# z as a fourth kind of the seven-product scheme, and a quarter of the off-diagonal low parts on GpSimd, in a two-layer encoder trunk on one core

## The chip, the cores and the metric

One core of a Trainium2 chip. The engines named below are TensorE (PE, with PEld for its weight loads), VectorE (DVE), ScalarE (ACT), GpSimd (POOL) and SyncE (SP, whose queue issues the DMAs of this kernel). The metric is the device time of one execution in microseconds, as the median of three runs. All work is on this core; there is no other core to wait for.

## The reference, cut to what matters

A stream of 2048 tokens with 1024 channels goes through two layers. Layer 0 is a pooling mixer with a gate; from its result keys and values are made once. Layer 1 is a strictly causal stick-breaking attention with 16 heads of 64, whose output is multiplied by SiLU(z). In layer 1 q and z come from one projection of the same normed stream:

```python
h = rms_norm(x, b_norm[j])
q, z = jnp.split(h @ b_w_in[j], 2, axis=-1)          # 1024 channels each
q = rms_norm(split_heads(q), b_q_norm[j])
o = stick_breaking_attention(q, k_sh, v_sh)          # keys s < t only
x = x + (o * jax.nn.silu(z)) @ b_w_out[j]
x = x + (p[i] @ ple_w[i]) * jax.nn.sigmoid(x @ ple_gate_w[i])
```

Everything is fp32. The kernel reaches that accuracy with fp32r matmuls: each operand is split into a high part (a cast to fp32r, on ACT) and a low part (the fp32 value minus the high part, on VectorE or GpSimd), and each product takes three matmuls: high by high, high by low, low by high.

## The kernel before, in words

**Tiling.** The stream lies transposed, channels in the partitions, in four chunks (0 to 3) of 512 tokens. A row is 128 channels x 512 tokens; a chunk of 1024 channels has eight rows. A product of a chunk with a 1024 x 1024 weight is 8 x 8 tiles x 3 matmuls = 192 matmuls of 128x128 by 128x512.

**Stages, in the order in which they run.** Mixer of chunk 0 (`mixed_part`), its gate (`gated_part`), mixer of chunk 1, gate of chunk 1, then `pair_part(0, 1)`, which makes v, k and q of both chunks; then the first attention (`attend` over chunks 0 and 1, 48 slots); gate of chunk 3; `pair_part(2, 3)`; the second attention (chunks 2 and 3, 112 slots); the last chunk's output (`post(3)`). What is left over runs as a filler stream between the matmuls of the attentions: in the first one z of chunks 0 and 1 (`z_part`, `gate_z`, 192 matmuls for each chunk), the mixer and gate of chunk 2 and the mixer of chunk 3 (`beside_first`); in the second one z of chunks 2 and 3 and the outputs of chunks 0 to 2 (`beside_second`). A number of filler matmuls for each half step of the attention (`share`) spreads them evenly.

**The seven products.** For v, k and q of two chunks the kernel takes the 2x2 block product with seven multiplications instead of eight (`job`): products p1 to p7 with 48 matmuls each and 12 multiply-adds of tiles behind them, so 336 matmuls for each kind and pair of chunks instead of 384. It needs mixtures of the weight's four blocks and of the stream's four blocks. The stream's mixtures (`prefill`, `build`) are made at the start of each pair. The weight's mixtures are made once, in `mixtures()`, as a side job of chunk 1's mixer: a step loads four blocks of 128x512 on SP's queue into four `mx` tiles, ACT scales them by the gain, VectorE or GpSimd by turns makes four differences in place, and four stores put them into DRAM (`mixed[kind, name]`). The `mx` tiles share eight buffers (`ppt`) with the attention's `pp` tiles. A kind has four steps. The results of a kind are handed on by `evacuate`, `valued` (v) and `keyed` (k, q; heads are normed there and transposed on TensorE).

**Weights on their way to TensorE.** All weight tiles of dense products come as units: a DMA into `wraw`, a cast into `wpair` on ACT (L208), a low part, and for some a store of the split form, which later uses load again. `take` and `plan` set which unit is loaded ahead of which.

**A half step of the attention.** A slot is one head of one chunk against one key chunk, taken from the diagonal down. `front` makes the scores of a block of 128 queries by 512 keys (ACT's sigmoid into `pp`, L1141, then a running product along the keys as a scan on VectorE, L1145); `turn`, three half steps later, transposes a block of 128 keys by 512 queries on TensorE into the bank `psa`, takes the high part by a cast on ACT (`at`, L1163) and the low part by a subtract on VectorE (L1165); `gather`, one half step on, multiplies both parts with the values (`pso`). Each half step has two of each, and a slot takes two half steps.

**What sets the order.** In the pairs and the attentions (`hold`) TensorE's instructions keep the order of the code; all else is ordered by a scheduler, and each engine runs its list in that order. SP's queue is in order, too. Work that is put off (`after`, `late`, `store(n)`) falls n matmuls later in the list.

## Time and profile before

| | value |
|---|---|
| median of 3 runs | 2713.84 us (2712.88 to 2716.44) |
| profiled execution | 2712.43 us, span 2710.6 us, mean granted clock 0.992 |
| TensorE matmul | 2645.2 us busy, 98% |
| TensorE weight load | 2202.2 us, 81% |
| VectorE | 2040.2 us, 75% |
| ScalarE | 1464.7 us, 54% |
| GpSimd | 903.6 us, 33% |
| DMA | 630.76 MB, 233 GB/s on average |

How to read it: the rows of a stage give start and end in microseconds from the span's start, then the busy time and the number of instructions of PE, PEld, DVE, ACT, POOL and SP's DMA issues. A row of the timeline gives start, duration, engine, line, operation, out<-in and shapes, how many in a row (x), and in square brackets the wait ahead of it and what ended it. A row of the waits reads: who waited, at which line, for whom; total us, times, longest one.

### The profile page before, as it was taken

Reading aid. Unit: us, or ns where it says so; the run is one execution under the profiler, and the core shown is the slowest. Engines: PE = TensorE matmul, PEld = TensorE weight load, DVE = VectorE, ACT = ScalarE, POOL = GpSimd, SP = SyncE. Lnnn points to the kernel's source line nnn. Section 1 sums busy time; section 2 is a strip of 40 time slices with the busy share of each in tenths; the row PEclk is TensorE's granted clock in tenths of the full one; section 3 lists DMA queues with packets and bytes.
Section 4 is the critical chain, followed back from the end, with each engine's and each line's share of the span. In section 5 each row is a group of like instructions: output and inputs, shape, how many; then the busy total and the mean of one; then the engine's idle time right before and its main releaser. Section 6 shows DMA issues by size and latency. Waiting matters only on the chain.

```text
span 2710.6 us, 38493 instructions
## 1 busy us (share of the span) xinstructions
PE 2645.2 (98%) x13118; PEld 2202.2 (81%) x13118; DVE 2040.2 (75%) x2663; ACT 1464.7 (54%) x2906; POOL 903.6 (33%) x685
## 2 busy tenths in 40 slices
PE   9999999999899999999999999999999999999999
PEld 7888887788678887888878787888888888888887
DVE  6744768567857878797576668889988888899842
ACT  5442354466676547555444656666665555555531
POOL 1235554576643414542445766110100100010000
PEclk9999999999999999999999999999999999999999
DMA  6768995957998766866459678755665565556564
GB/s 250 266 231 282 364 315 158 309 170 238 360 353 302 267 229 205 295 219 238 151 158 296 189 221 292 274 188 185 204 230 175 187 214 183 183 171 233 169 201 155
DMA packets 315361, 630.76 MB, mean 233 GB/s; under 512 B 47646, under 2 KB 80414, under 8 KB 315164
## 3 DMA queue, kind: packets, MB, share of 16 engines
q1 hardware_dynamic: 314588, 627.51, 69.2%
q8 instruction: 104, 1.70, 0.3%
q14 instruction: 93, 0.76, 0.1%
q10 hardware_dynamic: 576, 0.79, 0.1%
HBM read 463.03 MB, written 165.15 MB: 232 GB/s over the span
## 4 chain that ended last, share of the span: by engine, by line
PE 57%; DVE 13%; DMA 6%; issue 4%; POOL 4%; ACT 2%; SPq 1%; DVEq 0%; ACTq 0%; POOLq 0%
PE psd L51 26%; PE pso L51 8%; PE psl L51 7%; PE psa L55 7%; DVE pp L1145 4%; PE total L51 4%; PE own L51 4%; DVE at L1165 2%; POOL rq L181 1%; DVE wpair L210 1%; DMA wraw<-in_gate_a_dram 1%; PE pst L55 1%; DMA xw<-x2d 1%; DVE us L576 1%; DMA wraw<-in_w_kv_dram 1%
## 5 line engine op out<-in xcount | busy, mean ns | idle before, releaser
L1145 DVE TENSOR_TENSOR_SCAN pp<-pp,floor 128x512 f32<-128x512 f32 (+3 forms) x640 | 739.5, 1193 | 2.2 <-ACT pp L1141 2.1
L51 PE MATMUL psd<-x,wpair 128*128 128x512 f32 x2304 | 574.0, 395 | 1.3 <-ACT sg L718 0.6
L1163 ACT CAST at<-psa 128x512 fp32r<-128x512 f32 (+3 forms) x640 | 303.9, 525 | 386.2 <-PE psa L55 384.7
L51 PEld LDWEIGHTS psd<-x,wpair 128*128 128x128 f32 x2304 | 433.5, 190 | 94.3 <-ACT sg L718 1.0
L1165 DVE TENSOR_TENSOR at<-psa,at 128x512 fp32r<-128x512 f32 (+3 forms) x640 | 360.0, 600 | 146.6 <-ACT at L1163 145.0
L51 PE MATMUL psd<-xp,wpair 128*128 128x512 f32 x1392 | 337.3, 392 | 1.8 <-DMA wpair<-wf 1.5
L51 PE MATMUL pso<-at,vv 128*128 128x512 f32 (+3 forms) x1280 | 319.3, 367 | 17.2 <-DVE at L1165 13.2
L1141 ACT ACTIVATE pp<-psl 128x512 f32<-128x512 f32 (+3 forms) x640 | 312.8, 549 | 4.1 <-PE psl L51 3.5
L51 PEld LDWEIGHTS psd<-xp,wpair 128*128 128x128 f32 x1392 | 258.7, 188 | 57.6 <-DMA wpair<-wf 1.9
L55 PE MATMUL psa<-ident,pp 128*128 128x128 f32 x2176 | 293.1, 274 | 4.9 <-DVE at L1165 3.7
L51 PEld LDWEIGHTS pso<-at,vv 128*128 128x128 f32 x1280 | 229.8, 188 | 78.7 <-DVE at L1165 29.1
L51 PE MATMUL total<-wpair,xs 128*128 128x512 f32 x1152 | 278.2, 397 | 3.4 <-DVE wpair L210 1.7
L55 PEld LDWEIGHTS psa<-ident,pp 128*128 128x128 f32 x2176 | 253.2, 141 | 33.7 <-DVE at L1165 5.3
L1188 POOL TENSOR_TENSOR os<-os,zt 128x512 f32<-128x512 f32 x32 | 51.0, 1593 | 683.5 <-ACT os L1187 674.4
L51 PE MATMUL psl<-kk,qa 128*128 128x512 f32 (+3 forms) x640 | 259.8, 410 | 3.7 <-ACT pp L1141 3.6
L51 PEld LDWEIGHTS total<-wpair,xs 128*128 128x128 f32 x1152 | 215.3, 190 | 52.5 <-DVE wpair L210 4.2
L210 DVE TENSOR_TENSOR wpair<-wraw,wpair 128x512 fp32r<-128x512 f32 x193 | 176.9, 938 | 98.2 <-ACT wpair L208 97.9
L51 PE MATMUL psl<-kk,qb 128*128 128x512 f32 (+3 forms) x640 | 235.6, 368 | 6.9 <-ACT qb L1108 6.9
L51 PE MATMUL own<-wpair,xs 128*128 128x512 f32 x864 | 209.0, 397 | 7.7 <-ACT qs L938 7.7
L51 PEld LDWEIGHTS own<-wpair,xs 128*128 128x128 f32 x864 | 162.3, 190 | 42.6 <-ACT qs L938 9.4
L51 PE MATMUL psd<-og,wpair 128*128 128x512 f32 x744 | 184.6, 390 | 0.0
L51 PE MATMUL psd<-mp,wpair 128*128 128x512 f32 x768 | 178.8, 390 | 0.0
(151 smaller groups left out, 3657.8 us busy)
## 6 DMA issues: line engine op xcount, KB each, us to landing
wpair<-once SPq DMA_DIRECT2D x288, 512.0 KB, 4.8
kk<-kd SPq DMA_DIRECT2D x160, 256.0 KB, 3.5
vv<-vd SPq DMA_DIRECT2D x160, 256.0 KB, 3.3
once<-wpair SPq DMA_DIRECT2D x48, 512.0 KB, 6.3
wpair<-wf SPq DMA_DIRECT2D x48, 512.0 KB, 5.7
xw<-x2d SPq DMA_DIRECT2D x72, 256.0 KB, 4.5
once<-kp SPq DMA_DIRECT2D x36, 512.0 KB, 4.6
wraw<-in_gate_a_dram SPq DMA_DIRECT2D x64, 256.0 KB, 3.2
```

The costliest lines, as they stand in the source:

```text
L51: return held_in_order(nc.tensor.matmul(*a, **k))
L55: return held_in_order(nc.tensor.transpose(*a, **k))
L181: G.tensor_tensor(out=out_ap, in0=ms, in1=neghalf[:, 0:w], op=ALU.pow)
L210: (V if state["solo"] or state["lo"] % 2 else G).tensor_tensor(out=pr[:, 1], in0=raw, in1=f(pr[:, 0]), op=ALU.subtract)
L576: V.tensor_tensor(out=us[:, lo:][:, ::-1], in0=cur[:, lo:][:, ::-1], in1=cur[:, lo - sh : n][:, ::-1], op=ALU.add)
L1141: A.activation(out=pp[:, r0:], in_=ps[:, :w], func=AF.Sigmoid, scale=-1.0)
L1145: V.tensor_tensor_scan(out=pp[:, r0:][:, ::-1], data0=pp[:, r0:][:, ::-1], data1=least, initial=1.0 if st["diag"] else st["carry"][j], op0 ...
L1163: A.copy(out=at[:, 0, cs], in_=pt[:, cs])
L1165: return lambda: V.tensor_tensor(out=at[:, 1, cs], in0=pt[:, cs], in1=f(at[:, 0, cs]), op=ALU.subtract)
L1188: G.tensor_tensor(out=os, in0=os, in1=zt, op=ALU.mult)
```

## The change

z becomes a fourth kind (`KINDS = "vkqz"`): its four products are made in the pairs by the seven-product scheme, with the weight tile as the stationary operand, and `opened` takes SiLU and stores it. `mixtures()` therefore has 16 steps instead of 12, spaced 35 matmuls apart instead of 46, still as a side job of chunk 1's mixer. `z_part`, `gate_z`, `reload` and `plan_z` go, and with them 384 filler matmuls from each attention, so `share` falls. `prep(2)` (loading chunk 2's stream, splitting it and summing its squares), which ran beside z of chunk 1, moves to the end of `pair_part(0, 1)`, with its low parts on VectorE; loads of the first chunk's heads for the outputs move to the end of `pair_part(2, 3)`. In chunks 2 and 3, in blocks off the diagonal, the low part of the fourth key block (kt == 3) is made by GpSimd from a copy of the bank that ACT takes into a `pp` tile that is done with. The value differences go from GpSimd to VectorE.

```diff
@@ -264
-    KINDS = "vkq"
+    KINDS = "vkqz"
...
     def plan_kinds():
         for kind in KINDS:
-            src, gain = {"q": (b_w_q, g_b), "k": (w_kv, g_kv), "v": (w_kv, g_kv)}[kind]
+            src, gain = {"z": (b_w_z, g_b), "q": (b_w_q, g_b), "k": (w_kv, g_kv), "v": (w_kv, g_kv)}[kind]
...
@@ -433
-            ck[nm] = row("acc") if nm == "acc1" else pool.tile([P, W5], F32, tag="acc", name="acc", bufs=1)
+            ck[nm] = row("acc") if nm == "acc1" and ck is not chunk[2] else pool.tile([P, W5], F32, tag="acc", name="acc", bufs=1)
@@ -530
-            split(pr, xin, G)
+            split(pr, xin, V if state["hold"] and state["solo"] else G)
...
-        if state["solo"]:
+        if not state["hold"]:
             ck["rb1"] = bcast(token_norm(ck["acc1"], "x"), "x")
             return
@@ -667
-                x1 = xr
+                x1 = row("x1")
                 if whole is not None:
-                    x1 = row("x1")
                     whole.append(x1)
@@ -741
     def differences(s, b, j, vr, vs):
-        G.tensor_tensor(out=vs, in0=vs, in1=vr, op=ALU.subtract)
+        V.tensor_tensor(out=vs, in0=vs, in1=vr, op=ALU.subtract)
@@ -811
-    def gate_z(s, acts):
...
+    def opened(s, half, m, zr):
+        sg = tmp("sg")
+        A.activation(out=sg, in_=zr, func=AF.Sigmoid)
+        V.tensor_tensor(out=zr, in0=zr, in1=sg, op=ALU.mult)
+        store(16, out=zd[s][m + 4 * half], in_=zr)
@@ -877
-        for name in ("p5", "p3", "p7", "p6", "p4"):
+        for name in ("p3", "p5", "p7", "p6", "p4"):
             sets[name] = [home(8 + i) if name == "p6" and i < 3 else pair("xs") for i in range(4)]
@@ -909
     def mixtures():
...
-            src, gain = {"q": (b_w_q, g_b), "k": (w_kv, g_kv), "v": (w_kv, g_kv)}[kind]
+            src, gain = {"z": (b_w_z, g_b), "q": (b_w_q, g_b), "k": (w_kv, g_kv), "v": (w_kv, g_kv)}[kind]
@@ -930
     def evacuate(c0, c1, kind, name, j, total, own, parts):
...
+            elif kind == "z":
+                opened(c, b, j, qs)
@@ -973
-                            T.matmul(ps, half_of(sets[name][i], xh)[:, tk], u[:, wh, 0],
+                            xs, w = half_of(sets[name][i], xh), u[:, wh, 0]
+                            if kind == "z":
+                                xs, w = w, xs
+                            T.matmul(ps, xs[:, tk], w,
@@ -981
-    def reload(s):
...
@@ -1015
-    def pair_part(c0, c1):
+    def pair_part(c0, c1, back, width):
...
-        back = reload(c0)
...
-            if n >= total - 96 and n % 10 == 0:
+            if n >= total - width and n % 12 == 0:
                 next(back, None)
@@ -1052
-        yield from mixed_part(1, mixtures(), 46)
+        yield from mixed_part(1, mixtures(), 35)
         yield from gated_part(1, prefill(0), 26)
-        yield from pair_part(0, 1)
+        yield from pair_part(0, 1, prep(2), 140)
+
+    def head_loads():
+        for n in range(1, KT + 1):
+            load_heads(0, n)
+            yield
 
     def beside_first():
-        yield from z_part(0, reload(1))
-        yield from z_part(1, prep(2))
         yield from mixed_part(2)
...
     def middle():
         yield from gated_part(3, prefill(2), 26)
-        yield from pair_part(2, 3)
+        yield from pair_part(2, 3, head_loads(), 100)
 
     def beside_second():
-        yield from z_part(2, reload(3))
-        yield from z_part(3)
         for c in range(NSUB - 1):
             yield from post(c)
@@ -1162
-        return lambda: V.tensor_tensor(out=at[:, 1, cs], in0=pt[:, cs], in1=f(at[:, 0, cs]), op=ALU.subtract)
+        if st["c"] < 2 or st["diag"] or kt < 3:
+            return lambda: V.tensor_tensor(out=at[:, 1, cs], in0=pt[:, cs], in1=f(at[:, 0, cs]), op=ALU.subtract)
+        raw = st["a"][3][0]
+        A.copy(out=raw, in_=pt)
+        return lambda: G.tensor_tensor(out=at[:, 1], in0=raw, in1=f(at[:, 0]), op=ALU.subtract)
@@ -1267
-    attend(0, FIRST, beside_first(), lambda n: (1776.0 - 44) / (2 * FIRST + LAG_G + 1))
+    attend(0, FIRST, beside_first(), lambda n: (1392.0 - 44) / (2 * FIRST + LAG_G + 1))
...
-           lambda n: (1680.0 - 44) / (2 * (len(slots) - FIRST) + LAG_G + 1))
+           lambda n: (1296.0 - 44) / (2 * (len(slots) - FIRST) + LAG_G + 1))
@@ -1315
-        "b_w_z": blocks(b_in[:, 1024:], 256),
+        "b_w_z": blocks(b_in[:, 1024:], 512),
```

In numbers of instructions: TensorE issues 96 matmuls fewer. ACT gets 80 copies of a bank and 16 scalings of `mx` more, and 32 casts of x fewer. VectorE gives up 80 low parts of `at` and takes 32 value differences; GpSimd the other way round. SP issues 32 loads of z's mixtures, 16 loads of blocks and 16 stores more, 48 loads and 16 stores of split z units and 32 reloads of the stream fewer.

Three places in the order. In the rows `x3` stands for three in a row.

First, ACT at the start of chunk 1's gate (L208 is the cast of a weight unit, L188 the cast of a high part, `mx<-mx,gains` the scaling of a mixture step's blocks; the gate's products go to `psd` and its first output is the sigmoid `sg<-psd`). Before:

```order
L921 ACTIVATE mx<-mx,gains 128x512
L188 CAST x_3642<-xr 128x512
L921 ACTIVATE mx<-mx,gains 128x512 x3
L208 CAST wpair<-wraw 128x512 x3
L921 ACTIVATE mx<-mx,gains 128x512 x2
L208 CAST wpair<-wraw 128x512
L921 ACTIVATE mx<-mx,gains 128x512 x2
L188 CAST x_3693<-xr 128x512
L188 CAST ple<-pin 128x512 x2
L208 CAST wpair<-wraw 128x512 x2
L718 ACTIVATE sg<-psd 128x512 x2
```

After, from behind the first activations of z's second step (the casts of the gate's first three units stand some rows ahead of this):

```order
L188 CAST xs<-xw 128x512
L884 ACTIVATE mx<-mx,gains 128x512
L188 CAST xs<-xw 128x512
L884 ACTIVATE mx<-mx,gains 128x512
L188 CAST xs<-xw 128x512
L884 ACTIVATE mx<-mx,gains 128x512
L188 CAST xs<-xw 128x512
L884 ACTIVATE mx<-mx,gains 128x512 x4
L208 CAST wpair<-wraw 128x512 x2
L884 ACTIVATE mx<-mx,gains 128x512 x4
L208 CAST wpair<-wraw 128x512 x4
L709 ACTIVATE sg<-psd 128x512
```

The casts of the gate's fourth unit and of the first ple unit, which stood among the last steps of q, now stand behind the first of the two full sets of four `mx` activations (z's second step), and the next four casts behind the second (z's third step).

Second, SP's queue at the same place (L70 is a store, L917 or L880 the load of a mixture step's block, L225 the load of a weight unit). Before:

```order
L917 DMA mx<-in_b_w_q_dram 128x512
L225 DMA wraw<-in_gate_a_dram 128x512
L70 DMA mixedqp_383<-mx 128x512
L917 DMA mx<-in_b_w_q_dram 128x512
L70 DMA mixedqp_381<-mx 128x512
L917 DMA mx<-in_b_w_q_dram 128x512
L70 DMA mixedqp_384<-mx 128x512
L225 DMA wraw<-in_gate_a_dram 128x512
L917 DMA mx<-in_b_w_q_dram 128x512
L225 DMA wraw<-in_ple_a_dram 128x512
L225 DMA wraw<-in_gate_a_dram 128x512 x2
L70 DMA x2d_0_141<-sg 128x512
```

After:

```order
L70 DMA mixedqp_384<-mx 128x512
L70 DMA mixedzp_386<-mx 128x512
L70 DMA mixedzp_387<-mx 128x512
L880 DMA mx<-in_b_w_z_dram 128x512
L70 DMA mixedzp_385<-mx 128x512
L880 DMA mx<-in_b_w_z_dram 128x512 x2
L70 DMA mixedzp_388<-mx 128x512
L880 DMA mx<-in_b_w_z_dram 128x512 x5
L70 DMA mixedzp_386<-mx 128x512
L225 DMA wraw<-in_gate_a_dram 128x512
L70 DMA mixedzp_387<-mx 128x512
L225 DMA wraw<-in_gate_a_dram 128x512
```

Where two gate loads stood among q's last step, two gate loads now stand behind stores of z's mixtures (`mixedzp`), which go out only when the step's differences are made.

Third, ACT and GpSimd in the second attention (L1120 is the new line of the cast of `at`, L1125 the copy of the bank, L1126 GpSimd's subtract). ACT before:

```order
L1163 CAST at<-psa 128x512 x2
L1141 ACTIVATE pp<-psl 128x512 x2
L1163 CAST at<-psa 128x512 x2
L1141 ACTIVATE pp<-psl 128x512 x2
L1163 CAST at<-psa 128x512 x2
L1141 ACTIVATE pp<-psl 128x512 x2
```

ACT after:

```order
L1120 CAST at<-psa 128x512 x2
L1125 COPY pp<-psa 128x512
L1098 ACTIVATE pp<-psl 128x128
L1098 ACTIVATE pp<-psl 128x256
L1120 CAST at<-psa 128x512 x2
L1098 ACTIVATE pp<-psl 128x384
L1098 ACTIVATE pp<-psl 128x512
L1120 CAST at<-psa 128x512 x2
L1125 COPY pp<-psa 128x512
L1098 ACTIVATE pp<-psl 128x512 x2
```

GpSimd after:

```order
L1126 TENSOR_TENSOR at<-pp,at 128x512 x4
L1149 TENSOR_TENSOR os<-os,zt 128x512
L189 TENSOR_TENSOR op<-os,op 128x512
L1126 TENSOR_TENSOR at<-pp,at 128x512 x4
L1149 TENSOR_TENSOR os<-os,zt 128x512
L189 TENSOR_TENSOR op<-os,op 128x512
```

The copy follows the two casts of its half step, ahead of the next sigmoids; on GpSimd the subtracts stand in the same list as the products with z (`os<-os,zt`) and the low parts of the outputs.

58 lines of the change are left out of this document (7 added, 51 removed).

## The prediction

> **What bounds the kernel now.** I read the page first, then the busy time stage by stage, then who TensorE waits for.
>
> ```profile
> PE 2645.2 (98%) x13118; PEld 2202.2 (81%) x13118; DVE 2040.2 (75%) x2663; ACT 1464.7 (54%) x2906; POOL 903.6 (33%) x685
> ...
> 229.50:364.30 134.80, 133.29 (x593) 109.69 (x592) 83.72 (x95) 44.90 (x72) 66.25 (x59) 1.00 0.95 348
> 364.30:419.80 55.50, 55.07 (x241) 44.74 (x240) 47.09 (x46) 31.49 (x56) 36.80 (x25) 1.00 0.80 257
> 688.70:1337.40 648.70, 623.98 (x3157) 522.91 (x3156) 491.49 (x633) 378.13 (x806) 269.20 (x206) 0.99 0.75 263
> 1651.00:2607.00 956.00, 941.82 (x5058) 793.92 (x5057) 850.43 (x1041) 574.55 (x1190) 98.40 (x61) 0.99 0.61 201
> ...
> PE pso L51 <- DVE at L1165: 13.2, 16, 1.9
> PE pst L55 <- DVE at L1165: 5.9, 6, 2.4
> PE pst L51 <- POOL acc L441: 3.8, 2, 2.4
> ```
>
> A stage's row gives its length, then the busy time of PE, PEld, DVE, ACT and POOL, the clock, the DMA share and GB/s. TensorE is the bound nearly everywhere; its longest entry of waits is 13.2 us in the whole run. Two stages have a second resource close behind. In 229.5 to 364.3 (chunk 1's mixer, where the weight mixtures are made) the DMA engines are 95% busy; in 1651 to 2607 (second attention) DVE is at 850.4/956 = 89%. These are the places where this change adds work or takes cover away. A filler matmul costs its start-to-start time:
>
> ```profile
> 413.04 5.60 PE L51 MATMUL psd<-x,wpair 128*128 128x512 f32 x24
> 418.48 1.53 PE L51 MATMUL psd<-ple,wpair 128*128 128x512 f32 x6
> ```
>
> 24 starts in 5.44 us: 0.227 us each.
>
> **The matmuls.** z took 192 matmuls for each of four chunks, 768. As a kind it takes 7 products x 48 = 336 for each pair of chunks, 672. 96 fewer at 0.227: **-21.8 us**. They leave the attentions (384 each) and come to the pairs (336 each); in the pairs TensorE has 259.8 of 268.9 us now, and z there needs one sigmoid and one product per block and no heads to be normed, so it should run at the same rate.
>
> **The mixtures: a new wait in chunk 1's gate.** Four more steps (16 loads of 256 KB and 16 stores of the same size) must pass SP's queue, ACT and the eight pp buffers. How such steps run now, in the third kind (first loads of its four steps, last load, first and last store of the fourth), then ACT and PE beside them:
>
> ```profile
> 340.23 0.33 SPq L917 DMA_DIRECT2D mx<-in_b_w_q_dram  x1
> 352.74 0.33 SPq L917 DMA_DIRECT2D mx<-in_b_w_q_dram  x1
> 357.88 1.19 SPq L917 DMA_DIRECT2D mx<-in_b_w_q_dram  x2
> 372.79 0.42 SPq L917 DMA_DIRECT2D mx<-in_b_w_q_dram  x1
> 378.54 0.40 SPq L917 DMA_DIRECT2D mx<-in_b_w_q_dram  x1
> 384.46 0.38 SPq L70 DMA_DIRECT2D mixedqp<-mx  x1
> ...
> 363.11 1.39 ACT L921 ACTIVATE mx<-mx,gains 128x512 f32<-128x512 f32 x2 [0.24 <-DMA mx<-in_b_w_q_dram]
> 364.41 1.65 ACT L208 CAST wpair<-wraw 128x512 fp32r<-128x512 f32 x3
> 373.75 0.62 ACT L188 CAST x<-xr 128x512 fp32r<-128x512 f32 x1 [4.64 <-DVE xr L674]
> 364.33 9.68 PE L51 MATMUL psd<-x,wpair 128*128 128x512 f32 x42
> ...
> L921 ACT ACTIVATE mx<-mx,gains x48: 706/722/727, 248.2 to 385.1; 128x512 f32<-128x512 f32 x48
> L924 POOL TENSOR_TENSOR mx<-mx x6: 1295/1494/1744, 263.7 to 381.7; 128x512 f32<-128x512 f32 x6
> DMA to landing us min/median/max: 2.3/6.4/8.1
> ```
>
> A step reuses the buffers of the step two before, so its loads wait for those stores to land: first to third step 17.7 us, second to fourth 20.1 us. The gate (from 364.33) needs its first three weight units split by ACT; that happens at 364.41, right behind mixture work that ACT had waited for. It is in time by nothing. In the new order of ACT the casts of the gate's fourth unit and of the first ple unit stand behind the second z step's four activations, and SP issues two more gate loads only behind a store of that step. TensorE reaches the fourth unit after 36 matmuls: 364.33 + 36 x 0.227 = 372.5. When is it there? Bounds: ACT's own work between the cast of the gate's last input and this cast is 12 activations of 0.72, four xs casts and two ple casts at 0.6, 12.2 us; were the input cast at 365.6 (1.3 after 364.33), the unit would come at 378.4, 6 us late, with no load ever late. At the other end the third kind's fourth step stays where it is (last load 378.54) and z's second step comes one cycle of 20.1 later, lands 6.4 on and needs 0.72 + 0.6: 406.4, 34 us late. In the new order fewer gate loads stand ahead of that fourth step; I give it 8 us for this: 398.4, **+26 us** on TensorE's path (6 to 34). The nearest rows are the cycles measured in this same stage, so I stay near that end. Checked by volume: 32 transfers of 256 KB are 8.4 MB, 24 us at the 348 GB/s that the stage before moves at 95% busy, while the gate's own stage has only a fifth of its 55 us free. The Trainium skill (DMA: Bandwidth & Descriptors, Specifications) puts a core's share of HBM at about 358 GB/s; by that figure the volume would be an estimated 23 us, no other result.
>
> **The low part on GpSimd.** 80 times the low half of the fourth key block leaves DVE; ACT copies the bank a second time and GpSimd subtracts. The rows show a half step of the second attention with the two after it, then a scan pair without and with a GpSimd instruction beside it, then both kinds of DVE work in the groups:
>
> ```profile
> 2422.19 1.03 PE L55 MATMUL psa<-ident,pp 128*128 128x128 f32 x8
> 2422.88 1.08 ACT L1163 CAST at<-psa 128x512 fp32r<-128x512 f32 x2 [1.82 <-PE psa L55]
> 2423.99 1.76 PE L51 MATMUL psd<-og,wpair 128*128 128x512 f32 x7
> 2425.59 1.09 PE L51 MATMUL pso<-at,vv 128*128 128x512 f32 x4
> 2426.52 1.03 PE L55 MATMUL psa<-ident,pp 128*128 128x128 f32 x8
> 2429.47 1.09 PE L51 MATMUL pso<-at,vv 128*128 128x512 f32 x4
> ...
> 2421.18 2.44 DVE L1145 TENSOR_TENSOR_SCAN pp<-pp,floor 128x512 f32<-128x512 f32 x2
> 2437.04 3.44 DVE L1145 TENSOR_TENSOR_SCAN pp<-pp,floor 128x512 f32<-128x512 f32 x2
> 2437.86 1.54 POOL L189 TENSOR_TENSOR x<-x,x 128x512 fp32r<-128x512 f32 x1 [20.83 <-ACT x L188]
> ...
> L1145 DVE TENSOR_TENSOR_SCAN pp<-pp,floor 128x512 f32<-128x512 f32 x352 | 455.8, 1329 | 0.2 <-ACT pp L1141 0.2
> L1165 DVE TENSOR_TENSOR at<-psa,at 128x512 fp32r<-128x512 f32 x352 | 227.1, 682 | 77.2 <-ACT at L1163 76.0
> ```
>
> Two things happen. First, latency. The casts end at 2423.96, the copy 0.54 later (half of 1.08), the subtract 1.3 to 1.74 after that: 2425.8 to 2426.2. The matmul that reads it is the fourth of the next gather, 2425.59 + 3 x 0.23 = 2426.28, and it comes earlier now: the filler per half step falls from (1680-44)/229 = 7.14 matmuls to (1296-44)/229 = 5.47, by 0.38 us, to 2425.90. So GpSimd is from 0.1 early to 0.3 late. The 80 are the blocks off the diagonal: 16 heads of chunk 2 with two such key chunks, 16 of chunk 3 with three. For 32 of them (16 heads in each) the scores that stand between the transposes and gather are those of a diagonal block, which are shorter; there gather follows the transposes after 2.95 instead of 3.40 us, and it is 0.35 to 0.75 late. Second, DVE: a GpSimd instruction lengthens a scan pair from 2.44 to 3.44 us. Between that 1.0 and, when it falls into a gap, 0, against 0.68 saved, DVE gains 54 us at best and loses 26 at worst over the 80. TensorE's stage shrinks to 956 - 384 x 0.227 = 869 us, DVE's 850 to between 796 and 876. I take 48 x 0.05 + 32 x 0.4 = **+15 us** (0 to 40) of waits for GpSimd and none for DVE. The Trainium skill (SBUF — State Buffer, Who interferes with whom) says of the port pair that VectorE and GpSimd share that whoever starts first holds it for its whole instruction when the VectorE instruction has two SBUF inputs, as the scan has; the row (1.0 of the 1.54 us added) bears that out in the main, and by the full rule DVE would lose about 80 x 1.5 - 54 = 66 us, an estimate, and become the bound.
>
> **The rest.** The transposes of q's heads no longer fall into the starts of the attentions, where they waited for DVE (the 5.9 us row): -6 (0 to -12, with what those late heads delayed). Chunk 2's squares are now summed at the end of a pair, where TensorE waits for GpSimd's sum as the 3.8 us row does twice: +2. First attention: DVE's 491 us less about 20 stand against 649 - 87 = 562, 84% instead of 76%: +3 (0 to 8). Value differences on DVE, 32 x 0.68 = 22 us, lie in the pairs where DVE has 188.6 of 268.9 us; they take GpSimd off, cost nothing by themselves, and if DVE were late the totals' adds would be next.
>
> Sum: -21.8 + 26 + 15 - 6 + 2 + 3 = +18, on the profiled execution's 2712.4: 2730.6. The median of the runs is 1.4 above it, within their spread; I say **2730 us**, 0.6% slower.
>
> **Rivals.** (1) The mixtures keep their distance: no wait in the gate beyond 6 us because z's steps are ready early. Then 2730 - 20 = 2710, no change, and with GpSimd in time too 2695. For it: mixture loads stand about one step further ahead in the new order. Against: the buffer cycle. It decides if z's second step loads before 366 (6.4 + 0.7 ahead of 372.5). Chance 0.30 in all, of which 0.20 below 2708 by one or both terms. (2) DVE becomes the bound of the second attention: scans blocked for about 1 us by each of 80 subtracts, DVE at 876 us and its present idle time before casts (77 us) only halved, 876 + 38 = 914 instead of 869 + 15: 2730 + 30 = 2760. It decides once a subtract costs the scans more than 0.68. Chance 0.13. (3) The matmul rate of the pairs falls with z, DVE adding what ACT copies: 10 us of pair waits more, 2740; inside the range, 0.05. That the scheme does not save: the new order holds 672 z matmuls, so no.
>
> **Chances.** Forecast 0.52, rival 1 0.30, rival 2 0.13, rival 3 0.05. Range: 2694 (both terms at their low ends, rival 1's 2695) to 2756 (gate at 34, GpSimd at 30). 0.2%, 5.4 us, is about what runs of this kernel tell from no change. Faster (below 2708): rival 1's 0.20 and 0.04 of the forecast's low side, 0.24. Within: 0.17. Slower: 0.59.
>
> **What would show it.** Right: in the profile after, one TensorE gap of 15 to 30 us about 372 us in, ended by ACT's cast of wpair, while ACT waits for mx loads; waits of pso for GpSimd's at, some 30 of 0.3 to 0.5 us; no pst wait at the attentions' starts. Wrong: a gate stage as long as now (55 us), or pso waiting for DVE instead.

## The result and the profile after

The changed kernel takes 2785.0 us (median of 4 runs, 2779.4 to 2787.1) against 2714.5 before: ratio 1.0256, 95% interval 1.0238 to 1.0274. It is 2.6% slower; forecast were 2730 us and a range of 2694 to 2756. The profiled execution took 2779.4 us with a span of 2777.6, 67.0 more than before. By stages, each from the first matmul of its kind to that of the next (an attention from its first scores to its last product with the values; the last output ends with the last matmul; the middle column is the time before with the matmuls that the change adds or takes, at 0.227 us):

| stage | before | by matmuls alone | after | beyond |
|---|---|---|---|---|
| up to chunk 1's gate | 364.3 | 364.3 | 363.2 | -1.1 |
| gate of chunk 1 | 55.5 | 55.5 | 82.9 | +27.4 |
| pair of chunks 0, 1 | 268.8 | 345.1 | 360.3 | +15.2 |
| first attention | 640.6 | 553.4 | 536.2 | -17.2 |
| gate of chunk 3 | 60.7 | 60.7 | 70.6 | +9.9 |
| pair of chunks 2, 3 | 261.0 | 337.3 | 344.2 | +6.9 |
| second attention | 954.5 | 867.3 | 917.4 | +50.1 |
| last output | 100.0 | 100.0 | 97.7 | -2.3 |

The last column adds up to 88.9; 96 matmuls less make -21.8; together 67.1. One thing moved that the middle column leaves out: 32 small transposes of q's heads that stood in each attention now stand in the pair before it, 36 with those of the squares in the first one. They start 0.109 us apart, so 3.5 to 3.9 us of each pair's excess are no loss, and each attention has as much less to do. The engines on the page of the kernel after, then its windows for three stages with an excess, then who TensorE waits for:

```profile
PE 2648.4 (95%) x13022; PEld 2176.6 (78%) x13022; DVE 2103.9 (76%) x2662; ACT 1546.8 (56%) x3042; POOL 921.5 (33%) x710
```

```profile
363.20:446.20 83.00, 57.00 (x242) 46.03 (x242) 61.28 (x61) 42.02 (x71) 51.06 (x34) 0.86 0.85 279
446.20:806.50 360.30, 341.97 (x1542) 279.39 (x1541) 237.11 (x324) 195.31 (x342) 167.11 (x131) 0.97 0.70 215
1757.40:2674.80 917.40, 873.72 (x4645) 708.58 (x4644) 839.65 (x935) 592.05 (x1228) 182.53 (x122) 1.00 0.54 173
```

```profile
PE pso L51 <- DVE at L1123: 34.5, 54, 2.5
PE psd L51 <- ACT wpair L208: 24.6, 1, 24.6
PE pst L51 <- POOL acc L433: 14.3, 3, 11.2
PE pso L51 <- POOL at L1126: 11.1, 22, 1.1
PE psd L51 <- ACT x L188: 8.8, 1, 8.8
```

Three single waits of 24.6, 11.2 and 8.8 us stand out, one in each gate and one at the end of a pair; the waits of pso in the attentions are many and short. DVE is busier than before (2103.9 against 2040.2 us) although 80 low parts left it and only 32 differences and z's work in other places came (for z's products among others 42 more low parts of weight units and 32 more adds of results, by the records of both traces).

The first single wait, in the gate of chunk 1 (timeline after; SPq is SP's queue):

```profile
363.24 8.32 PE L51 MATMUL psd<-x,wpair 128*128 128x512 f32 x36
388.78 5.77 SPq L880 DMA_DIRECT2D mx<-in_b_w_z_dram  x5
392.92 1.41 ACT L884 ACTIVATE mx<-mx,gains 128x512 f32<-128x512 f32 x2 [2.94 <-DMA mx<-in_b_w_z_dram]
395.49 1.12 ACT L208 CAST wpair<-wraw 128x512 fp32r<-128x512 f32 x2
396.14 2.08 PE L51 MATMUL psd<-x,wpair 128*128 128x512 f32 x4 [24.58 <-ACT wpair L208]
```

After the 36 matmuls of the gate's first three units TensorE stands until ACT casts the fourth at 395.5, behind the activations of z's second step, which wait for its loads. That is the predicted place, releaser and size (398.4 forecast). The path is the predicted one, too: the last load of q's fourth step was issued at 368.3 instead of 378.5 (the prediction gave 8 us for this), that of z's second step 20.5 us later (forecast 20.1), and it landed after 6.0 (forecast 6.4). Ahead of these activations ACT also waited 7.1 us in four pieces for VectorE's scaling of the stream (`xw`), which the prediction's path doesn't have.

The other two, at the end of the first pair and in the gate of chunk 3:

```profile
776.70 0.40 SPq L521 DMA_DIRECT2D xin<-in_x_dram  x1
784.67 0.62 ACT L188 CAST xh<-xin 128x512 fp32r<-128x512 f32 x1 [6.36 <-DMA xin<-in_x_dram]
785.96 1.26 POOL L433 TENSOR_TENSOR acc<-acc,sq 128x512 f32<-128x512 f32 x1 [7.25 <-ACT sq L432]
787.28 1.87 PE L51 MATMUL pst<-ones,acc 128*128 128x1 f32 x8 [11.20 <-POOL acc L433]
...
1357.12 0.62 ACT L208 CAST kp<-kraw 128x512 fp32r<-128x512 f32 x1 [4.70 <-DMA kraw<-in_b_w_out_dram]
1363.47 0.62 ACT L188 CAST x<-x 128x512 fp32r<-128x512 f32 x1
1364.14 1.22 PE L51 MATMUL psd<-x,wpair 128*128 128x512 f32 x2 [8.82 <-ACT x L188]
```

GpSimd's last sum is named, but it had waited itself: the last block of chunk 2's stream, issued at 776.7, reached ACT only at 784.7. In the gate ACT waited 4.7 us for an output weight (`kraw`), and the cast of the gate's last input stood behind it in ACT's list.

Each of the three waits costs more than its length. In these windows the third number from the end is the granted clock; the first two rows are the matmuls right behind the first wait and those after them, the others those right behind the second and the third:

```profile
396.14:399.50 3.36, 3.36 (x8) 2.68 (x9) 3.36 (x3) 3.36 (x7) 3.20 (x3) 0.50 0.55 184
399.50:410.00 10.50, 10.50 (x47) 8.66 (x47) 9.24 (x12) 6.31 (x12) 4.16 (x3) 1.00 0.94 295
787.28:792.10 4.82, 4.82 (x15) 4.19 (x16) 1.29 (x2) 0.71 (x3) 1.22 (x2) 0.50 0.48 160
1364.14:1368.90 4.76, 4.76 (x11) 3.79 (x12) 4.76 (x4) 2.13 (x4) 3.53 (x3) 0.50 0.80 288
```

For 3.4 to 4.8 us after TensorE goes on the granted clock is 0.50, and 128x512 matmuls start 0.43 us apart instead of 0.227. The 8 behind the first wait took 3.5 us instead of 1.8, the 11 behind the third 4.8 instead of 2.5. So about 2 us of each excess come on top of the wait.

Two half steps of the second attention, one beside full scores and one beside the scores of a diagonal block:

```profile
2426.15 0.66 DVE L1123 TENSOR_TENSOR at<-psa,at 128x512 fp32r<-128x512 f32 x1
2426.26 0.59 ACT L1125 COPY pp<-psa 128x512 f32<-128x512 f32 x1 [1.03 <-DVE pp L1102]
2426.92 1.27 POOL L1126 TENSOR_TENSOR at<-pp,at 128x512 fp32r<-128x512 f32 x1 [2.95 <-PE psd L51]
2427.38 3.07 DVE L1102 TENSOR_TENSOR_SCAN pp<-pp,floor 128x512 f32<-128x512 f32 x2 [0.57 <-ACT pp L1098]
2428.24 0.51 PE L51 MATMUL pso<-at,vv 128*128 128x512 f32 x1 [0.65 <-POOL at L1126]
...
2434.63 0.59 ACT L1125 COPY pp<-psa 128x512 f32<-128x512 f32 x1 [0.46 <-DVE pp L1102]
2435.29 1.28 POOL L1126 TENSOR_TENSOR at<-pp,at 128x512 fp32r<-128x512 f32 x1 [7.10 <-ACT pp L1125]
2435.43 2.01 DVE L1102 TENSOR_TENSOR_SCAN pp<-pp,floor 128x128 f32<-128x128 f32 x2 [0.25 <-ACT pp L1098]
2436.63 0.50 PE L51 MATMUL pso<-at,vv 128*128 128x512 f32 x1 [0.65 <-POOL at L1126]
```

Three things can be seen in each: ACT's copy waits for a pair of scans, VectorE waits for the sigmoids behind the copy, and the scans that start during the subtract are long (a pair of 128x512 took 2.44 us without; the second half step's pair is one of 128x128 and one of 128x256, 0.43 and 0.66 us without). Which of them costs was the question of most experiments.

### The profile page after: what moved, and what is told of

Its sections match the earlier page's. It is cut to its first block, busy times and chain, and to the rows that moved or that the text cites. A ratio compares the mean times of both kernels' runs of the same rounds, so it can differ in the third digit from the quotient of the medians.

```text
span 2777.6 us, 38771 instructions
## 1 busy us (share of the span) xinstructions
PE 2648.4 (95%) x13022; PEld 2176.6 (78%) x13022; DVE 2103.9 (76%) x2662; ACT 1546.8 (56%) x3042; POOL 921.5 (33%) x710
## 4 chain that ended last, share of the span: by engine, by line
PE 49%; DVE 15%; issue 7%; DMA 5%; ACT 5%; POOL 3%; SPq 0%; POOLq 0%; DVEq 0%; ACTq 0%
PE psd L51 18%; PE total L51 9%; DVE pp L1102 8%; PE own L51 6%; PE pso L51 5%; PE psa L55 5%; PE psl L51 5%; DVE at L1123 2%; POOL at L1126 2%; DMA wraw<-in_gate_a_dram 1%; ACT at L1120 1%; PE pst L55 1%; DMA xin<-in_x_dram 1%; ACT pp L1125 1%; ACT pp L1098 1%
## 5 line engine op out<-in xcount | busy, mean ns | idle before, releaser
L1102 DVE TENSOR_TENSOR_SCAN pp<-pp,floor 128x512 f32<-128x512 f32 (+3 forms) x640 | 790.9, 1271 | 41.5 <-ACT pp L1098 41.2
L1120 ACT CAST at<-psa 128x512 fp32r<-128x512 f32 (+3 forms) x640 | 303.2, 524 | 326.3 <-PE psa L55 324.8
L51 PE MATMUL psd<-x,wpair 128*128 128x512 f32 x1536 | 386.7, 396 | 33.4 <-ACT wpair L208 24.6
L51 PE MATMUL pso<-at,vv 128*128 128x512 f32 (+3 forms) x1280 | 345.1, 377 | 51.6 <-DVE at L1123 34.5
L1123 DVE TENSOR_TENSOR at<-psa,at 128x512 fp32r<-128x512 f32 (+3 forms) x560 | 310.2, 585 | 92.3 <-ACT at L1120 90.9
L51 PEld LDWEIGHTS psd<-x,wpair 128*128 128x128 f32 x1536 | 291.9, 191 | 96.7 <-ACT wpair L208 25.0
L1126 POOL TENSOR_TENSOR at<-pp,at 128x512 fp32r<-128x512 f32 x80 | 104.6, 1308 | 533.8 <-ACT pp L1125 499.5
L210 DVE TENSOR_TENSOR wpair<-wraw,wpair 128x512 fp32r<-128x512 f32 x211 | 188.2, 910 | 98.9 <-ACT wpair L208 98.3
L208 ACT CAST wpair<-wraw 128x512 fp32r<-128x512 f32 x228 | 136.5, 617 | 86.1 <-DMA wraw<-in_gate_a_dram 34.1
```

Source lines behind the costliest of these rows:

```text
L51: return held_in_order(nc.tensor.matmul(*a, **k))
L208: held_split(A.copy(out=pr[:, 0], in_=raw))
L210: (V if state["solo"] or state["lo"] % 2 else G).tensor_tensor(out=pr[:, 1], in0=raw, in1=f(pr[:, 0]), op=ALU.subtract)
L1102: V.tensor_tensor_scan(out=pp[:, r0:][:, ::-1], data0=pp[:, r0:][:, ::-1], data1=least, initial=1.0 if st["diag"] else st["carry"][j], op0 ...
L1120: A.copy(out=at[:, 0, cs], in_=pt[:, cs])
L1123: return lambda: V.tensor_tensor(out=at[:, 1, cs], in0=pt[:, cs], in1=f(at[:, 0, cs]), op=ALU.subtract)
```

## The experiments

Ratios are to the kernel before, which ran beside each (2716 to 2718 us in these series), with their 95% interval. Stage times are of the profiled executions.

### Does GpSimd's part cost the 50 us of the second attention?

```diff
-        if st["c"] < 2 or st["diag"] or kt < 3:
+        if True:
```

> The changed kernel with all low parts of at back on VectorE (no copy of the bank, no GpSimd subtract); all else as changed. It asks whether the 50 us that the second attention has beyond 954.5 - 87.2 = 867 us come from GpSimd's part at all. Theory A (GpSimd's part costs it, by the copy's wait or by what it does to the scans): second attention 917 -> 875 to 888 us, total 2742 to 2755, TensorE's waits there for VectorE 5 to 15 us. Rival B (with 384 fewer filler matmuls VectorE is the bound in any case: 850 us of work, its idle time for casts unchanged at about 77): 915 to 930 us, total 2780 to 2800. The three other places (gate of chunk 1 with 24.6 us, end of the first pair 11.2, gate of chunk 3 8.8) stay as they are by both.

2745.1 us, ratio 1.0097 (1.0064 to 1.0130); the stage takes 879.0 instead of 917.4. Theory A: GpSimd's part costs 38.4 us. The other 11.7 above 867.3 are there without it, and TensorE's waits for VectorE, 21.4 us there, are above theory A's 5 to 15. The other three waits stayed (gate of chunk 1 84.3, pair 358.5, gate of chunk 3 70.9). The groups of VectorE in that stage, first this kernel, then the changed one:

```profile
L1102 DVE TENSOR_TENSOR_SCAN pp<-pp,floor 128x512 f32<-128x512 f32 x352 | 455.3, 1328 | 0.1
L1102 DVE TENSOR_TENSOR_SCAN pp<-pp,floor 128x256 f32<-128x256 f32 x32 | 21.3, 664 | 0.0
L1102 DVE TENSOR_TENSOR_SCAN pp<-pp,floor 128x128 f32<-128x128 f32 x32 | 13.8, 432 | 0.2 <-ACT pp L1098 0.2
```

```profile
L1102 DVE TENSOR_TENSOR_SCAN pp<-pp,floor 128x512 f32<-128x512 f32 x352 | 489.3, 1423 | 25.6 <-ACT pp L1098 25.4
L1102 DVE TENSOR_TENSOR_SCAN pp<-pp,floor 128x128 f32<-128x128 f32 x32 | 40.9, 1277 | 6.5 <-ACT pp L1098 6.5
L1102 DVE TENSOR_TENSOR_SCAN pp<-pp,floor 128x256 f32<-128x256 f32 x32 | 25.3, 789 | 0.0
```

VectorE gives up 80 x 0.68 = 54 us and pays 34.0 + 27.1 + 4.0 = 65.1 us in longer scans, and it waits 32 us for sigmoids where it had waited under 1.

### Is it the copy's wait for the scan?

```diff
-        raw = st["a"][3][0]
+        raw = st["a"][2][0]
```

> The changed kernel with the copy of the bank put into the pp tile of the third block of queries instead of the fourth. In the trace after, ACT's copy often starts right when a pair of scans has ended. Theory A1: it waits for the scan of the next key chunk's fourth block, which takes the tile's first column as its carry; the third block's carry is read one scan (1.3 to 1.5 us) earlier, so copy and subtract come that much sooner: the wait of gather for GpSimd (11.1 us, and 34.5 on its weight loads) falls under 3 us, ACT's wait for the scans (15.2) goes, second attention 917 -> 885 to 900, total 2753 to 2768. Theory A2 (the scans are lengthened by GpSimd's subtract beside them, 1.33 to 1.42 us each on average, and VectorE is the bound): nothing moves, 912 to 920, total 2779 to 2788. Rival B of the run beside it gives the same as A2.

2785.5 us, ratio 1.0250 (1.0223 to 1.0277); stage 916.5. ACT's wait ahead of the copy fell from 15.2 us to nothing that is listed and TensorE's for GpSimd from 11.1 to 5.4, but its waits for VectorE rose from 30.8 to 36.7. A1 was wrong: an earlier copy brings nothing by itself.

### The subtract alone, the copy alone, and the part in the kernel before

`pool_beside` (all low parts on VectorE; GpSimd's subtract beside them):

```diff
-        A.copy(out=raw, in_=pt)
-        return lambda: G.tensor_tensor(out=at[:, 1], in0=raw, in1=f(at[:, 0]), op=ALU.subtract)
+        def low():
+            V.tensor_tensor(out=at[:, 1], in0=pt, in1=f(at[:, 0]), op=ALU.subtract)
+            G.tensor_tensor(out=raw, in0=raw, in1=f(at[:, 0]), op=ALU.subtract)
+        return low
```

> The kernel with all low parts back on VectorE (second attention 879.0 us) and, beside the 80 low parts concerned, a GpSimd subtract of the same size on a pp tile and at whose result nobody reads; no copy of the bank. It measures what GpSimd's instruction alone does to VectorE's work. From the busy times: with GpSimd's part VectorE is busy 839.6 us in that stage with 80 low parts fewer, without it 819.5; so 20.1 + 80 x 0.68 = 74.5 us, 0.93 a subtract, would be what the subtracts add to the other VectorE instructions. Theory C1 (the subtract lengthens the scans beside it, and that is the cost): VectorE's busy time 819 -> 880 to 900, scans of 128x512 at about 1.42 us on average (1.33 or below without), stage 925 to 960 us, total 2790 to 2825, slower than the change itself. Theory C2 (the cost comes from the copy standing ahead of the sigmoids on ScalarE): stage 878 to 888, total 2745 to 2755.

`copy_beside` has the copy and VectorE's low part:

> The kernel with all low parts back on VectorE (second attention 879.0 us) and the 80 copies of the bank on ScalarE as in the change, into the same pp tile, which nobody reads. It measures the copy's place in ScalarE's list, ahead of the next sigmoids, alone. Theory C1: nothing but a little of the copy's 0.6 us shows, stage 879 to 886, total 2745 to 2752. Theory C2: sigmoids come 0.6 us and the copy's wait for the scan later, VectorE waits for them as it did in the change (32.1 us for pp by ScalarE against 0.6), stage 900 to 917, total 2766 to 2785.

`before_pool` puts the changed lines of `turn` into the kernel before:

> The kernel before with one part of the change alone: in chunks 2 and 3 the fourth key block's low part off the diagonal by a copy on ScalarE and a subtract on GpSimd. The second attention keeps its 384 filler matmuls for z (954.5 us). Theory C1: VectorE's busy time 850 - 54 + 74 = 870 us and its idle time stays near 77: 947, just inside the stage, so waits show only here and there: 955 to 968 us, total 2714 to 2730. Theory C2, and the prediction's first thought (latency of the GpSimd path by 0.1 to 0.4 us at 80 places): 960 to 990. If it is below 950 the part has a gain of its own where the cover is there.

| kernel | time, ratio (interval) | second attention | VectorE busy | 128x512 scan | waits for sigmoids |
|---|---|---|---|---|---|
| all on VectorE | 2745.1, 1.0097 | 879.0 | 819.5 | 1.328 | 0.6 |
| + subtract | 2753.7, 1.0124 (1.0099 to 1.0149) | 885.6 | 846.9 | 1.372 | 0.6 |
| + copy | 2750.8, 1.0124 (1.0101 to 1.0146) | 885.1 | 826.5 | 1.333 | under 2.5 |
| changed kernel | 2785.0, 1.0256 | 917.4 | 839.6 | 1.423 | 32.1 |
| before + GpSimd's part | 2732.0, 1.0057 (1.0037 to 1.0077) | 970.6 | 866.0 | 1.416 | 39.5 |

Neither C1 nor C2 holds: each piece alone costs 6 us, the two with VectorE's low part gone cost 38. With VectorE's own low part in its list the sigmoids come in time, and 0.91 us of each subtract (1.37) run beside such a low part, whose source is in PSUM and which stays at 0.68 us, and 0.48 beside scans; in the change 0.91 of 1.31 run beside scans (sums over the records of both traces; scans of 128x128 take 0.73 us on average here, 1.28 in the change). So `pool_beside` gave the subtract another neighbour than the change does; its scans lost 0.34 us a subtract (27.1 / 80). The part is a loss of 16 us in the kernel before, too, where nothing else is changed.

### Where in the half steps it is lost

`ff_only` takes GpSimd's part away at the 32 places beside a diagonal's scores; `nowait` lets TensorE not wait for GpSimd at any of the 80; `defer` has the part at key chunks above 0 and the reading matmul behind the scores. Key chunk 0 is a head's last. The code is shortened.

```diff
# ff_only
-        if st["c"] < 2 or st["diag"] or kt < 3:
+        if st["c"] < 2 or st["diag"] or kt < 3 or slots.index((st["c"], st["h"], 0)) - st["i"] == 1:
# nowait
-        T.matmul(po[:, cs], vv[:, kt, :], at[:, 1, cs], ...)
+        T.matmul(po[:, cs], vv[:, kt, :], at[:, int(st["c"] < 2 or st["diag"] or kt < 3), cs], ...)
# defer
+        if st["c"] < 2 or st["diag"] or st["last"] or kt < 3: low()
+        else: behind.append(low)          # issued after the fronts
```

> The changed kernel with GpSimd's part kept at 48 of the 80 places: not where the scores made in the same half step are those of a diagonal block (key chunk 1 of each head, 32 places; there VectorE makes the low part again). By half steps, from one transposes' start to the next: where a full block's scores stand beside a GpSimd low part the half step takes 4.22 us in the change and 4.14 with all on VectorE, where a diagonal's stand 4.39 and 3.85, and the two half steps after those 4.18 and 3.40 against 3.92 and 3.11. Theory D (the loss sits at the 32 places, since the half step is short there): second attention 917 -> 880 to 886, total 2746 to 2753. Rival E (80 places cost alike, 38.4 / 80 = 0.48 us each): 917 - 32 x 0.48 = 902, total 2768.

> The changed kernel with copy and GpSimd subtract at all 80 places, but the matmul that should read GpSimd's low part reads the high part again, so TensorE does not wait for GpSimd; the low part's share is left out of the result at these places. Theory F (latency: cast, copy, subtract in a chain of about 3.2 us behind the transposes, longer than the short half step leaves): half steps beside a diagonal's scores 4.39 -> 3.85 to 3.95, second attention 917 -> 880 to 890, total 2745 to 2758. Rival G (the scans of 128x128 and 128x256 meet the subtract and run 1.28 and 0.79 us on average, and ScalarE's sigmoids come later: VectorE is late, not GpSimd): second attention above 905, total 2770 or more.

> The changed kernel with GpSimd's part at 48 places, all with key chunks above 0 (the 32 beside a diagonal's scores among them), and there the matmul that reads the low part put behind the scores of its half step, some 1.5 to 2.2 us later in TensorE's list; where it is the last of a head (key chunk 0, 32 places) VectorE makes the low part. Theory F: GpSimd is in time everywhere and VectorE has 33 us less to do: second attention 917 -> 868 to 882, at or below the 879.0 with all on VectorE. Rival G: the scans are still met and the sigmoids late: the half steps beside a diagonal's scores stay above 4.1 us, second attention 890 or more.

`nowait_late` is nowait with the copy behind the sigmoids in ACT's list:

> As the run in which TensorE reads the high part again instead of GpSimd's low part (that share is left out of the result), with ScalarE's copy of the bank now behind the sigmoids of its half step instead of ahead of them. The two half steps after a head's last key chunk took 4.21 and 3.41 us there, 3.92 and 3.11 with all on VectorE; VectorE waited 58 times for a sigmoid, 30.8 us in all, and the 128x512 scans took 1.423 us on average against 1.328. Theory H (the sigmoids behind the copy make VectorE late where it has no slack): VectorE's wait for sigmoids falls under 5 us and the two half steps to 3.9 to 4.0 and 3.1 to 3.2; second attention 895 -> 876 to 882, total 2745 to 2750. Theory I (the lengthened scans do it): the wait falls as well, but the scans stay at 1.42 and the half steps at 4.15 and 3.35 or more; second attention 890 or more.

Mean half step (us, from one transposes' start to the next), worked out from the matmul records of each trace; the two after a head's last key chunk are those that transpose the next head's diagonal block:

| half steps | all on VectorE | changed | ff_only | nowait | nowait_late | defer |
|---|---|---|---|---|---|---|
| beside a diagonal's scores (31) | 3.85 | 4.39 | 3.84 | 3.80 | 3.79 | 3.58 |
| first after a head's last key chunk (32) | 3.92 | 4.18 | 4.18 | 4.21 | 4.16 | 3.93 |
| second after it (32) | 3.11 | 3.40 | 3.41 | 3.41 | 3.41 | 3.14 |
| beside full scores, with kt 2, 3 (47) | 4.14 | 4.22 | 4.22 | 4.11 | 4.11 | 4.05 |
| with kt 0, 1 (79) | 4.07 | 4.06 | 4.04 | 4.06 | 4.04 | 4.21 |
| second attention | 879.0 | 917.4 | 898.5 | 895.0 | 892.4 | 878.5 |
| total | 2745.1 | 2785.0 | 2767.2 | 2763.9 | 2758.8 | 2750.3 |
| ratio | 1.0097 | 1.0256 | 1.0184 | 1.0170 | 1.0162 | 1.0125 |

The loss has two halves. 31 x 0.55 = 17 us lie beside a diagonal's scores. They go when TensorE does not wait there (nowait) and when it reads later (defer): latency, as theory F had it and as the prediction had it for these places. 32 x (0.26 + 0.29) = 17.5 us lie in the two half steps after each head's last key chunk; they stay in ff_only and nowait, and both D and F, which gave one cause for all, were half wrong. There TensorE waits for VectorE's own low parts: 16.7 us in these 64 half steps in the change, 6.1 with all on VectorE. The copy alone isn't it: in `copy_beside` they take 4.00 and 3.14 us. nowait_late tells the sigmoids from the scans there (its groups, then its waits in that stage):

```profile
L1104 DVE TENSOR_TENSOR_SCAN pp<-pp,floor 128x512 f32<-128x512 f32 x352 | 502.6, 1462 | 7.9 <-ACT pp L1098 6.7
```

```profile
DVE pp L1104 <- ACT pp L1098: 7.3, 25, 0.3
```

VectorE's wait for sigmoids fell from 30.8 to 7.3 us, and the half steps stayed at 4.16 and 3.41: theory I. What is left at these places is the subtract beside the scans, which are no shorter (those of 128x512 take 1.462 us; all forms together gain 61.9 us, 65.1 in the change). It is found by exclusion; the lengthening alone, with the low part gone from VectorE and no GpSimd work, wasn't tried. defer shows what the part is worth at best: with latency hidden and the 32 bad places on VectorE, 878.5 against 879.0.

### The three single waits

```diff
# nozmix: z's products p4 to p7 read q's mixtures
-        for kind in KINDS:
+        for kind in KINDS[:3]:
-        yield from mixed_part(1, mixtures(), 35)
+        yield from mixed_part(1, mixtures(), 46)
# keep_prep
-                if count % 42 == 0 and kept:
+                if count % 36 == 0 and kept:
-        yield from pair_part(0, 1, prep(2), 140)
+        yield from pair_part(0, 1, prep(2), 190)
```

> The changed kernel without z's weight mixtures: z's products p4 to p7 read q's mixtures instead, so the first 12 steps remain, 46 matmuls apart as before; z's values are left out of the computation by that, its matmuls are all there. The theory of the prediction: the gate of chunk 1 has its fourth unit in time, the gap of 24.6 us goes, the stage from gate to pair takes 55 to 60 us instead of 82.9, total 2756 to 2763. Rival: the gap has to do with the loads and buffers of the stream's mixtures for the pair or with the 1 us less of chunk 1's mixer, and stays above 12 us: 2773 or more. The second attention stays at 917 by both.

2762.8 us, ratio 1.0159 (1.0133 to 1.0186). The windows of chunk 1's gate:

```profile
363.56:424.46 60.90, 56.30 (x242) 44.47 (x241) 56.33 (x54) 33.65 (x59) 45.21 (x29) 1.00 0.79 270
```

The 24.6 us gap is gone: z's mixtures cost 22.0 us there. The stage is still 5.4 longer than before.

> The changed kernel with two numbers altered, in two stages that can be read apart. First, a kept weight of the outputs is split after every 36 filler matmuls of the first attention instead of 42: with 1348 fillers instead of 1732 only 32 of the 36 kept steps fit at 42, and the last four ran at the start of chunk 3's gate, where ACT waits 4.7 us for such a load with the gate's cast behind it. Theory: the gap of 8.8 us there goes, gate of chunk 3 70.6 -> 61 to 63 us. Rival: the gap is from the reload of the stream for the pair, which also moved; it stays above 5. Second, chunk 2's preparation starts 190 instead of 140 matmuls before the end of the first pair, 4 steps earlier. Theory: the last block of the stream (issued at 776.7, landed about 784.5) comes 11 us sooner and TensorE no longer waits 11.2 us for GpSimd's sum of squares: pair 360.3 -> 349 to 351 us. Rival: SP's queue or the buffers hold that load all the same, gap 6 us or more. Together by the theories 2785 - 9 - 10 = 2766, 2762 to 2770; by the rivals 2778 or more.

2773.0 us, ratio 1.0201 (1.0177 to 1.0226). The gate of chunk 3 took 62.0: its wait came from the kept steps, of which four had been left over. The pair stayed at 362.0 with a gap of 9.2 us. Half of that theory held: the last block of the stream landed at 773.3 instead of 784.7, 11 us sooner. But TensorE's sum of the squares is ordered 12 matmuls behind the last step, so it came sooner as well and stood waiting all the same.

### All causes taken away

`combo1`: all low parts on VectorE, a kept weight every 36 fillers, preparation at 190 with its sum 56 matmuls after the last step, and four of the 16 steps of mixtures beside chunk 0's gate (shortened):

```diff
-        yield from gated_part(0, prep(1), 22)
-        yield from mixed_part(1, mixtures(), 35)
+        mix = mixtures()
+        yield from gated_part(0, with_mixtures(prep(1), mix), 18)   # a step behind every other one of prep's
+        yield from mixed_part(1, mix, 46)
-        lag.append((time["now"] + 12, total))
+        lag.append((time["now"] + (56 if s == 2 else 12), total))
```

> The changed kernel with each cause found so far taken away: all low parts on VectorE; z's four steps of weight mixtures begun one stage earlier, beside the gate of chunk 0 (four steps there, twelve beside chunk 1's mixer, 46 matmuls apart), whose DMA engines are 59% busy over 56.6 us, so that 8.4 MB fit; a kept weight every 36 fillers; chunk 2's preparation 190 matmuls ahead of the pair's end with its sum of squares on TensorE 56 instead of 12 matmuls after the last step. By stages against the changed kernel: gate of chunk 1 82.9 -> 55 to 60, pair 360.3 -> 347 to 351, gate of chunk 3 70.6 -> 62, second attention 917 -> 879, the rest as it is: 2785 - 25 - 11 - 9 - 38 = 2702, 2694 to 2710, below the kernel before by 0.3 to 0.8%. Rival: z's volume of loads does not go away but moves the wait to the mixer of chunk 1 or the gate of chunk 0: those stages 190 -> 200 or more, total 2712 or more.

2714.7 us, ratio 0.9989 (0.9977 to 1.0001), above the forecast and in the rival's range. Second attention 877.3, gate of chunk 3 60.4, pair 350.5 with 1.1 us left of its wait: against `keep_prep` the pair has a greater distance between last load and sum, and the low parts, which also changed, leave a wait of 9.1 us in `lows_v`. But chunk 1's gate began at 368.1 and took 65.4.

`combo2` lets a step of mixtures follow each of prep's (every 11 matmuls one or the other), and x1 of chunks 1 and 3 stay in the loaded row:

> The kernel with all causes taken away, mended in two places that its profile showed: z's steps of mixtures alternate with chunk 1's preparation beside the gate of chunk 0 without delaying it (there TensorE waited 3.8 us for the cast of the last block), and the gate's input x1 of chunks 1 and 3 stays in the buffer of the loaded row, as in the kernel before, instead of taking one of the eleven rows that the stream's mixtures need too. Theory: start of chunk 1's gate 368 -> 364 us; gate of chunk 1 65.4 -> 56 to 60, since without any mixtures of z it took 60.9 with the new x1 and 55.5 with the old; total 2714.7 -> 2701 to 2708, 0.3 to 0.6% under the kernel before. Rival: the gate's 65 us are from the volume of loads (DMA 77% there) and x1 has no part: gate 63 or more, total 2709 or more.

2709.7 us, ratio 0.9968 (0.9955 to 0.9981), 2 us above the forecast. The gate of chunk 1 took 54.4, DVE 46.15 us in it instead of 57.83. The trace shows what x1's place has to do with it: with x1 in one of the eleven rows, the eight scalings of chunk 0's stream that open the pair's mixtures (`xw`, also in rows) run at 390 to 406 us, in the gate, and take 11.2 us of DVE there; with x1 in the loaded row they run at 252 to 267, as in the kernel before (250 to 259). Not all of it was gained: the pair behind took 355.3 instead of 350.5. The start of that gate did not get better (369.8).

`combo3` spaces z's steps 44 matmuls apart and keeps x1 in the loaded row for chunk 1 only:

> The last combined kernel with two more mends from its profile: z's steps of mixtures stand 44 matmuls apart beside the gate of chunk 0 (there TensorE waited 4.2 us for VectorE's low part of a ple unit that stood behind mixture work), and only chunk 1 keeps its gate's input in the loaded row's buffer; chunk 3 takes a row again, since its gate with the following pair took 409.0 us so and 405.5 with a row. Theory: start of chunk 1's gate 369.8 -> 365 to 367, gate of chunk 3 with its pair 409 -> 405.5, total 2709.7 -> 2700 to 2706. Rival: the loads of z's mixtures cost chunk 0's gate its 4 to 5 us wherever they stand in it: 2705 to 2710.

2708.3 us, ratio 0.9972 (0.9962 to 0.9981), 0.28% faster than the kernel before (2717.4 in that series). Gate of chunk 3 with its pair 407.0, but chunk 1's gate begins at 370.9 and takes 58.9 us, the pair behind it 349.6. Gate and pair together took 415.9, 409.7 and 408.5 us in the three combined kernels, so the two later ones gain 6 to 7 us there; x1's place, the main difference, wasn't changed alone. The rival held: chunk 1's gate begins at 368.1, 369.8 and 370.9 in them against 364.3 before, so four more steps beside chunk 0's gate cost 4 to 7 us wherever they stood in it.

`vs_pool` is the changed kernel with the value differences back on GpSimd:

> The changed kernel with the value differences back on GpSimd, in the pairs. The prediction costed their move to VectorE at nothing. Theory: pair 360.3 and 344.2 us stay within 2 us, total 2783 to 2788. Rival: VectorE was late with the totals' adds in v's part of the pairs, and each pair gets 3 to 5 us shorter: 2775 to 2779.

2780.4 us, ratio 1.0243 (1.0224 to 1.0261); pairs 362.0 and 343.6, both within 2 us: no effect to be seen there, as costed. The total lies between the two forecasts.

## Why the prediction was wrong, point by point

The direction held, the size did not: +18 forecast, +67 in the profiled executions. The step that failed is that of the low part on GpSimd, which saw no waits for VectorE; besides it three terms were at nothing or nearly so (cover, squares, kept steps).

- **The matmuls (-21.8).** Right: 13118 - 13022 = 96 fewer, and in combo3, where the other causes are mostly gone, the pair of chunks 0 and 1 takes 349.6 against 345.1 by matmuls alone, of which 3.9 are the transposes that moved there.
- **The mixtures (+26).** Right: +27.4, a gap of 24.6 at the named unit. 22.0 of the stage's excess are z's mixtures (nozmix); the other 5.4 are put down to the row for x1 (combo2), which the prediction did not cost. That the sum met the forecast within 1.4 us is partly luck: x1 and about 1.7 us of half clock aren't in it.
- **The low part on GpSimd (+15): the term that failed.** It measured 38.4, near the end of its own range of 0 to 40. The step that failed was to take waits for GpSimd and "none for DVE", after setting DVE's 796 to 876 us against a stage of 869. DVE's busy time came into that range (840), but a sum over the stage doesn't show single half steps: the two behind each head's last key chunk are 17.5 us longer in all, TensorE's waits for VectorE in them rise from 6.1 to 16.7 us, and by exclusion it is the lengthened scans that make VectorE late. The row from which the lengthening was bounded (scan pair 2.44 or 3.44) gave 0 to 1.0 us a place and was right: measured were (489.4 - 455.3) / 48 = 0.71 us at the 48 other places (ff_only) and 31.0 / 32 = 0.97 beside a diagonal's scores. That is not below the 0.68 saved, the point at which rival 2 was to decide; its 914 us for the stage came near the measured 917, in part by luck, since about half of the loss has another cause than it gave: latency. The Trainium skill (SBUF — State Buffer, Who interferes with whom) says that a VectorE instruction with two SBUF inputs and a GpSimd instruction that reads SBUF contend for a port pair, which one of them holds alone. The trace agrees: the scans lost 0.81 us for each subtract (65.1 / 80), and 0.91 of its 1.31 us lay beside a scan. The prediction's estimate by that rule took 1.5 us, the whole of another subtract, at every place, which was too much. The latency term was at its right places but too small: 17 us instead of 12.8 at the 32, 3.7 instead of 2.4 at the others.
- **Cover.** The prediction had no term for VectorE in the second attention without 384 fillers: 11.7 us with all low parts on VectorE, where TensorE's waits for its low parts rise from 8.4 to 21.4 us. That the missing fillers cause this wasn't tried by a run of its own.
- **The squares (+2).** +15.2 in the pair: 11.2 in one wait, 3.9 in the transposes that moved there. The row taken for it was GpSimd's sum; the wait was for the last load, which GpSimd's sum itself waited for.
- **No term at all: the kept steps.** They are counted in fillers (one in 42), and 384 fillers fewer leave four of 36 for the next gate: +9.9, a wait of 8.8 us and the half clock behind it. The prediction named `share`, but not what else counts fillers.
- **First attention (-6 and +3).** Better than thought: 17.2 us below its matmuls. TensorE's idle time there was 24.7 us before (615.8 of 640.6 busy) and is 13.1 after; 3.9 us are the transposes that moved out. The transposes' waits for VectorE (5.9 us in both attentions) are no longer in the list, as forecast. Why the rest of the idle time fell wasn't tried.
- **Value differences (0).** Right.
- **The signs.** Those of being right were there: the gap of 24.6 us, 22 waits for GpSimd's `at` of 0.5 us on average, no `pst` wait for VectorE. So was one of being wrong: `pso` waits 34.5 us for DVE, 13.2 before.

The sum by measured terms is -21.8 + 27.4 + 38.4 + 11.7 + 15.2 + 9.9 - 17.2, and +3.5 for the second pair (+6.9) and the two ends: 67.1. Of the 6.9, 3.5 are moved transposes, which the second attention no longer has; without them its cover costs 15.2 instead of 11.7.

## What to carry to other kernels

Here a subtract moved to GpSimd took no load off VectorE: 54 us saved, 65 added to the scans beside it, whose operands both lie in SBUF. Price what such a move adds to the work that stays, then the copy that feeds it, then the latency and the other engine's lateness where the half step is shortest, not over the stage. When filler is taken from a stage, look for everything that is paced by that filler: other work counted in it, and the slack of the engine that was second. A saving of 96 matmuls was worth 9 of its 22 us at the end, after the main waits that the extra preparation caused had been given a place of their own.

## What the runs showed of the hardware

Not expected was how even the exchange is between GpSimd and the scans, in both directions: whichever starts second loses nearly all of the time that the two share. In the kernel with all low parts on VectorE:

```profile
2427.16 2.44 DVE L1102 TENSOR_TENSOR_SCAN pp<-pp,floor 128x512 f32<-128x512 f32 x2
2427.24 3.46 POOL L189 TENSOR_TENSOR x<-x,x 128x512 fp32r<-128x512 f32 x1 [29.66 <-DVE at L1123]
```

A subtract that starts 0.08 us after a pair of scans takes 3.46 us instead of 1.28 and leaves the pair its 2.44; a subtract that had started 0.46 before the pair (the half step above) keeps its 1.27, 0.81 of it beside the pair, and the pair takes 3.07. A scan of 128x128 beside it went from 0.43 to 1.28 us on average.
